# Gate and up products with the activations held in the array and their result turned by TensorE

## The chip, the cores and the metric

The kernel runs on one core of a Trainium2 chip. The metric is device time of one execution, in microseconds (us), lower is better.

## The reference, cut to what matters

One decoder layer on 256 tokens of 2048 features, all in float32: a half-weighted feed-forward block (FFN1), a mixer with a recurrent and an attention branch, a second half-weighted feed-forward block (FFN2), and a last norm.

```python
def swiglu(x, w_gate, w_up, w_down):            # 2048x5504, 2048x5504, 5504x2048
    return (jax.nn.silu(x @ w_gate) * (x @ w_up)) @ w_down

x = x + 0.5 * swiglu(rms_norm(x, ffn1_norm[l]), ffn1_w_gate[l], ffn1_w_up[l], ffn1_w_down[l])
x = x + hybrid_mixer(rms_norm(x, mix_norm[l]), w_in[l], ...)
x = x + 0.5 * swiglu(rms_norm(x, ffn2_norm[l]), ffn2_w_gate[l], ffn2_w_up[l], ffn2_w_down[l])
return rms_norm(x, final_norm)
```

## The kernel before

All sizes are in tiles of P = 128: the 2048 features are KT = 16 tiles, the 5504 hidden features NF = 43 tiles, the S = 256 tokens two halves t of 128. C = 512 is a chunk of four tiles, and NC = 4 of them make 2048.

**Two parts for each number.** Every operand of a product is split into a high part, rounded for the array's fast float32 mode, and a low part, the rest. A product is three products: high by high, high by low, low by high. `split` makes the parts with one ScalarE (ACT) and one VectorE (DVE) instruction, at L72 and L73. An activation tile with both parts beside each other is an "hl" tile, 512 columns wide for each feature tile: the high parts of 256 tokens, then the low parts. Four slots of such tiles exist (`hlp`).

**Weights.** A `Stream` loads blocks of 128x1024 floats (512 KB) from memory over SyncE's queue into one of three `raw` buffers (L88) and splits each into `whi` and `wlo`, of which there are three as well. A `raw` buffer is free for the next load once its `wlo` is made.

**Two ways to multiply.** `part` (L116, L117) holds a 128x128 weight tile in the array and moves activations through it: `whi` with 512 columns (high and low at once), then `wlo` with 256. The result stands with features on the partitions, and `total` adds its two halves. `wide` (L138 to L140) holds activations in the array, 128 tokens of one feature tile, and moves 512 columns of weights: three matmuls for each half t. The result stands with tokens on the partitions, in one PSUM bank for each t. Five banks serve such products (`mm`), three other things (`aux`).

**Where each is used.** Gate and up products of both FFNs use `part`: for each of 43 hidden tiles j, 16 pairs of matmuls for gate and 16 for up, 1,376 pairs in each FFN. Each result is then scaled by the norm (`normed`), goes through Silu, is multiplied and split, and so becomes a tile of `h`, ready for the down product, which uses `wide`. Several products of the mixer, the merge of its branches and the output projection use `wide` too. Where a result with tokens on the partitions is needed with features there, `turned` (L164) transposes it on TensorE (PE), 128x128 at a time, eight for a chunk, and the two `split` halves are made from PSUM. These transposes are put off (`later`), and `wide` runs what was put off after its feature tile k = 7 (`AFTER`). In the merge, a chunk of gates goes through a tanh on ACT (L620) while the next chunk multiplies, is combined on DVE (L720, L721) and turned in the chunk after.

**The start of FFN1.** x comes in eight transfers of two feature tiles, among them the first blocks of gate and up weights. For tile j = 0 the gate product runs as x arrives: `ready1` scales and splits one tile of x (L75, L76). The sum of squares for the norm is made from x on ACT (`add_all`, L203), added up on DVE and over partitions on PE (L222), and the factor is spread over the partitions by another PE product (`rstd`, L262). A second copy of x, with tokens on the partitions (`xt`, from `x_rows`), is loaded at j = 4 in `prepare`, into the place that x had, and is added to the result of the down product. `prepare` also holds a small PE product (L418).

**Order of work.** The program's order gives priorities; a planner orders the instructions of each engine before the run, and takes an instruction that is ready in its plan ahead of an earlier one that is not. On the chip each engine and each queue then runs in that fixed order. `held` ties an instruction to a product so that it isn't planned too early.

Of the kernel before, what the change touches and what calls it, by code (L numbers as in the profile page):

```python
# [35 lines left out]
G = 8  # L36
T1 = 8
T2 = 5
AFTER = 7
BIG = 1e30  # L40
LOWEST = -3.0e38
C = 4 * P
NC = D // C
TAKEN = -3.4e38
# [3 lines left out]
def hybrid_layer(ctx: ExitStack, tc: tile.TileContext, a, out):  # L48
# [29 lines left out]
    class Stream:  # L78


        def __init__(self, src, width=P):
            self.src, self.width, self.ahead, self.left, self.at = src, width, [], [], 0

        def load(self, parts=1):
            raw = wraw.tile([P, G * P], F32, name="raw")
            n = G * P // parts
            for i in range(parts):
                nc.sync.dma_start(raw[:, i * n:(i + 1) * n], self.src[self.at, :, i * n:(i + 1) * n])  # L88
            self.parts = parts
            self.at += 1  # L90
            self.ahead.append(raw)

        def pop(self):
            if not self.left:
                if not self.ahead:
                    self.load()
                raw = self.ahead.pop(0)
                hi = wsp.tile([P, G * P], F32R, name="whi")
                lo = wsp.tile([P, G * P], F32R, name="wlo")
                n, self.parts = G * P // self.parts, 1  # L100
                for i in range(0, G * P, n):
                    split(hi[:, i:i + n], lo[:, i:i + n], raw[:, i:i + n])
                n = self.width
                self.left = [(hi[:, i:i + n], lo[:, i:i + n]) for i in range(0, G * P, n)]
            return self.left.pop(0)
# [26 lines left out]
    def wide(ps, w, k0, k1, kts, xs, apart=0):  # L132


        def half(t, k, hi, lo):
            x = xs(k)
            xh, xl = x[:, t * P:(t + 1) * P], x[:, S + t * P:S + (t + 1) * P]
            T.matmul(ps[t], xh, hi, start=(k == 0), stop=False)  # L138
            T.matmul(ps[t], xh, lo, start=False, stop=False)  # L139
            T.matmul(ps[t], xl, hi, start=False, stop=(k == kts - 1))  # L140
# [17 lines left out]
    def turned(src, dst):  # L158

        for i in range(0, 4, 2):  # L160
            pt = aux.tile([P, 2 * S], F32, name="aux")
            for j in range(2):
                for t in range(2):
                    T.transpose(pt[:, j * S + t * P:j * S + (t + 1) * P], src(t, i + j), ident)  # L164
            dst(i, pt.rearrange("p (j s) -> p j s", j=2))
# [25 lines left out]
    class Norm:  # L191


        def __init__(self, name):
            self.name, self.acc = name, None
            self.parts = const.tile([P, NC, 2], F32, name=name)

        def add_all(self, x, after):

            sq = hl_tile("sqs", F32, (P, KT, S))  # L200
            z = held(after)
            for c in range(0, KT, 4):
                A.activation(sq[:, c:c + 4, :], x[:, c:c + 4, :], AF.Square, bias=z)  # L203
            half = KT
            while half > 2:
                half //= 2
                V.tensor_tensor(sq[:, :half, :], sq[:, :half, :], sq[:, half:2 * half, :], op=ALU.add)
            self.acc = t1("sqsum")
            V.tensor_tensor(self.acc, sq[:, 0, :], sq[:, 1, :], op=ALU.add)
# [5 lines left out]
        def sums(self):  # L215

            n = tmp.tile([P, 8], F32, name="nv")
            v, s, r = n[:, 0:2], n[:, 2:4], n[:, 4:6]
            if self.acc is not None:
                ps = aux.tile([P, 2 * S], F32, name="aux")  # L220
                for t in range(2):
                    T.matmul(ps[:, t:t + 1], self.acc[:, t * P:(t + 1) * P], mean, start=True, stop=True)  # L222
                V.tensor_scalar(v, ps[:, :2], EPS, None, op0=ALU.add)
            else:
                q = self.parts
                V.tensor_tensor(q[:, 0:2, :], q[:, 0:2, :], q[:, 2:4, :], op=ALU.add)
                V.tensor_tensor(v, q[:, 0, :], q[:, 1, :], op=ALU.add)
                V.tensor_scalar(v, v, 1.0 / D, EPS, op0=ALU.mult, op1=ALU.add)
# [47 lines left out]
    mean = const.tile([P, 1], F32, name="mean")  # L276
    GP.memset(mean, 1.0 / D)
    warm = const.tile([P, 1], F32, name="warm")
    A.activation(warm, mean, AF.Copy)
# [5 lines left out]
    def ffn(wg, wu, wd, xhl, norm, finish, ready=None, early=None):  # L285
        hs = []
        r = None

        def evacuate(j, pg, pu):
            zg = normed(pg, r)  # L290
            sg = t1("sg")
            A.activation(sg, zg, AF.Silu)
            zu = normed(pu, r)
            h = t1("h")
            V.tensor_tensor(h, zu, sg, op=ALU.mult)
            t = hs[j // KT][:, j % KT, :]
            split(t[:, :S], t[:, S:], h)

        waiting = []
        for j in range(NF):  # L300
            if j % KT == 0:
                hs.append(hl_tile("h"))
            if j == 0:
                pg, pu = psum(), psum()
                for k0 in range(0, KT, G):
                    for k in range(k0, k0 + G):
                        if ready is not None:
                            ready(k)
                        part(pg, wg, k, k + 1, KT, whole(xhl))
                    part(pu, wu, k0, k0 + G // 2, KT, whole(xhl))  # L310
                    settle()
                    part(pu, wu, k0 + G // 2, k0 + G, KT, whole(xhl))
# [5 lines left out]
            waiting.append((j, pg, pu))  # L318
            if j == 0 and ready is not None:
                norm.add_all(xr, pg)  # L320
# [4 lines left out]
            if r is not None:  # L325
                for w in waiting:
                    evacuate(*w)
                waiting = []
# [6 lines left out]
    WG1, WU1, WD1 = Stream(a["wg1"]), Stream(a["wu1"]), Stream(a["wd1"], C)  # L335
    xr = big.tile([P, KT, S], F32, name="xr", tag="f16")
# [18 lines left out]
    def ready1(c):  # L355
        spread(x1hl, c, xr[:, c, :], G1)
# [3 lines left out]
    x2hl = xt = None  # L360

    def finish1(c, ps):
# [9 lines left out]
        def gains(i, pt):  # L372
            for j in range(2):
# [8 lines left out]
    def prepare(after):  # L382
        nonlocal xt
# [39 lines left out]
    ffn(WG1, WU1, WD1, x1hl, n1, finish1, ready=ready1, early=prepare)  # L423
# [288 lines left out]
    def merge(j):  # L712
# [10 lines left out]
        def parts(i, pt):  # L723
            n = 4 * j + i
            split(mg[:, n:n + 2, :S], mg[:, n:n + 2, S:], pt)
# [11 lines left out]
    def combine(c):  # L737
# [9 lines left out]
        def gains(i, pt):  # L747
            for j in range(2):
# [34 lines left out]
    ffn(Stream(a["wg2"]), Stream(a["wu2"]), Stream(a["wd2"], C), x3hl, n3, finish2)  # L783
# [19 lines left out]
def _rows(w):  # L803

    k, n = w.shape
    t = np.asarray(w).reshape(k // P, P, n // C, C).transpose(2, 0, 1, 3).reshape(-1, G // 4, P, C)
# [56 lines left out]
```

## Time and profile before

| | |
|---|---|
| median of 3 runs | 2333.41 us (2326.3 to 2334.53) |
| profiled execution | 2324.7 us |
| its span, first to last instruction | 2322.5 us |
| TensorE busy | 2302.0 us (99%) |
| VectorE, ScalarE busy | 1438.3 us (62%), 1140.5 us (49%) |
| mean granted TensorE clock | 0.998 of full |

The profile is one execution; the rows below are from it. A matmul's printed duration reaches into the next ones, since matmuls are pipelined, so what one costs in a stream is the distance between starts. On PE in the timeline, FFN1's gate and up products run from 5.46 to 501.38 us, its down product to about 743 us, the mixer to 1599.47 us, FFN2's gate and up to 2078.17 us, and its down product to the end.

### The profile page before, as it was taken

How to read it: one execution, taken by the hardware profiler on the slowest of the kernel's cores; microseconds unless marked ns; L12 is line 12 of the kernel's file. 1: busy time of each engine (PE TensorE's matmuls, PEld its weight loads, DVE VectorE, ACT ScalarE, POOL GpSimd, SP SyncE). 2: the span in 40 equal slices, each digit the busy share in tenths (PEclk: the TensorE clock that was granted, in tenths of full speed). 3: DMA queues.
4: the chain of work that ended last, by engine and by line, in shares of the span. 5: the costliest groups of instructions: out<-in, count | busy, mean ns of one | idle time of the engine just before them, and what ended most of it. 6: DMA issues, size and time to landing. Idle time of an engine off the chain costs nothing.

```text
span 2322.5 us, 31249 instructions
## 1 busy us (share of the span) xinstructions
PE 2302.0 (99%) x11916; PEld 1956.3 (84%) x11916; DVE 1438.3 (62%) x2061; ACT 1140.5 (49%) x1603; POOL 62.3 (3%) x122
## 2 busy tenths in 40 slices
PE   8999999999999999999999999999999999999998
PEld 7888888888888888888888888888888888888886
DVE  6766666654445687766677755555666666664444
ACT  6444444444444445566655544445544444444443
POOL 0000000000000011000000000000000000000000
PEclk9999999999999999999999999999999999999999
DMA  7555555556665644456666665565555555565554
GB/s 259 187 184 189 184 188 185 189 188 199 199 200 189 213 161 149 156 184 200 206 215 208 209 208 199 200 217 186 189 190 190 189 189 189 191 208 194 194 192 162
DMA packets 130166, 448.78 MB, mean 193 GB/s; under 512 B 14896, under 2 KB 21152, under 8 KB 129632
## 3 DMA queue, kind: packets, MB, share of 16 engines
q1 hardware_dynamic: 125856, 433.89, 56.1%
q0 software_dynamic: 3984, 12.82, 1.6%
q8 instruction: 93, 1.52, 0.3%
q14 instruction: 57, 0.47, 0.1%
q10 hardware_dynamic: 176, 0.08, 0.0%
HBM read 438.25 MB, written 8.41 MB: 192 GB/s over the span
## 4 chain that ended last, share of the span: by engine, by line
PE 97%; DVE 1%; ACT 1%; issue 0%; DMA 0%; SPq 0%; DVEq 0%; ACTq 0%
PE mm L116 36%; PE mm L117 18%; PE mm L138 13%; PE mm L140 13%; PE mm L139 13%; DVE wlo L73 0%; PE aux L164 0%; PE aux L496 0%; DMA raw<-in_wu 0%; PE aux L637 0%; PE aux L638 0%; ACT whi L72 0%; PE aux L559 0%; PE aux L580 0%; PE aux L587 0%
## 5 line engine op out<-in xcount | busy, mean ns | idle before, releaser
L73 DVE TENSOR_TENSOR wlo<-raw,whi 128x1024 fp32r<-128x1024 f32 (+2 forms) x807 | 989.2, 1226 | 789.0 <-ACT whi L72 786.1
L72 ACT ACTIVATE whi<-raw 128x1024 fp32r<-128x1024 f32 (+2 forms) x807 | 854.3, 1059 | 1101.5 <-PE mm L116 423.5
L116 PE MATMUL mm<-x1hl,whi 128*128 128x512 f32 x1376 | 489.3, 400 | 7.6 <-DVE x1hl L76 7.1
L116 PE MATMUL mm<-x3hl,whi 128*128 128x512 f32 x1376 | 477.6, 391 | 0.0
L117 PE MATMUL mm<-x1hl,wlo 128*128 128x256 f32 x1376 | 387.5, 282 | 2.0 <-DVE wlo L73 2.0
L117 PE MATMUL mm<-x3hl,wlo 128*128 128x256 f32 x1376 | 385.1, 280 | 0.0
L116 PE MATMUL mm<-x2hl,whi 128*128 128x512 f32 x960 | 344.0, 401 | 0.0
L116 PEld LDWEIGHTS mm<-x1hl,whi 128*128 128x128 f32 x1376 | 259.9, 189 | 73.3 <-ACT whi L72 6.4
L116 PEld LDWEIGHTS mm<-x3hl,whi 128*128 128x128 f32 x1376 | 257.3, 187 | 56.7 <-DVE x3hl L76 0.3
L117 PE MATMUL mm<-x2hl,wlo 128*128 128x256 f32 x960 | 269.6, 281 | 0.0
L138 PE MATMUL mm<-whi,h 128*128 128x512 f32 x688 | 267.9, 389 | 0.0
L140 PE MATMUL mm<-whi,h 128*128 128x512 f32 x688 | 267.7, 389 | 0.0
L139 PE MATMUL mm<-wlo,h 128*128 128x512 f32 x688 | 267.7, 389 | 0.0
L117 PEld LDWEIGHTS mm<-x1hl,wlo 128*128 128x128 f32 x1376 | 261.2, 190 | 3.2 <-DVE wlo L73 3.0
L117 PEld LDWEIGHTS mm<-x3hl,wlo 128*128 128x128 f32 x1376 | 260.0, 189 | 0.1
L116 PEld LDWEIGHTS mm<-x2hl,whi 128*128 128x128 f32 x960 | 180.4, 188 | 44.0 <-issue 1.1
L117 PEld LDWEIGHTS mm<-x2hl,wlo 128*128 128x128 f32 x960 | 181.3, 189 | 2.3 <-issue 0.7
L140 PEld LDWEIGHTS mm<-whi,h 128*128 128x128 f32 x688 | 129.2, 188 | 26.9
L139 PEld LDWEIGHTS mm<-wlo,h 128*128 128x128 f32 x688 | 129.2, 188 | 26.8
L138 PEld LDWEIGHTS mm<-whi,h 128*128 128x128 f32 x688 | 129.2, 188 | 26.6
L138 PE MATMUL mm<-whi,x2hl 128*128 128x512 f32 x288 | 115.4, 401 | 0.0
L140 PE MATMUL mm<-whi,x2hl 128*128 128x512 f32 x288 | 112.5, 391 | 0.0
(208 smaller groups left out, 2002.3 us busy)
## 6 DMA issues: line engine op xcount, KB each, us to landing
raw<-in_wu SPq DMA_DIRECT2D x172, 512.0 KB, 4.2
raw<-in_wd SPq DMA_DIRECT2D x172, 512.0 KB, 3.4
raw<-in_wg SPq DMA_DIRECT2D x171, 512.0 KB, 4.2
raw<-in_w_q SPq DMA_DIRECT2D x32, 512.0 KB, 3.5
raw<-in_w_rx SPq DMA_DIRECT2D x32, 512.0 KB, 3.5
raw<-in_w_ga SPq DMA_DIRECT2D x32, 512.0 KB, 3.4
raw<-in_w_rg SPq DMA_DIRECT2D x32, 512.0 KB, 3.8
raw<-in_w_pa SPq DMA_DIRECT2D x32, 512.0 KB, 3.8
```

The costliest lines, as they stand in the source:

```text
L72: A.activation(hi, src, AF.Copy)
L73: V.tensor_tensor(lo, src, hi.bitcast(F32), op=ALU.subtract)
L116: T.matmul(ps, hi, x, start=(k == 0), stop=False)
L117: T.matmul(ps[:, S:], lo, x[:, :S], start=False, stop=(k == kts - 1))
L138: T.matmul(ps[t], xh, hi, start=(k == 0), stop=False)
L139: T.matmul(ps[t], xh, lo, start=False, stop=False)
L140: T.matmul(ps[t], xl, hi, start=False, stop=(k == kts - 1))
```

## The change

Gate and up products of both FFNs are made with `wide`, four hidden tiles at once (chunks at j = 0, 4, ... 36, and one of three tiles, 384 columns, at j = 40). Their weights lie in memory in the order that `wide` wants, the last three tiles in arrays of their own (`wg1b` and so on). The result has tokens on the partitions, so that the norm's factor is one number per partition: Silu takes it as its scale on ACT, and one DVE instruction scales the up product and multiplies. `turned` then transposes the result into `h`.

The first chunk's gate and up products run side by side, two feature tiles of each in turn. Of x, two tiles and the first two blocks of weights are asked for, then two more tiles and a block; the rest follows as `opening1` is called. The copy with tokens on the partitions is loaded there as well, in four pieces, and the squares for FFN1's norm are made from it. The sum over partitions and the spreading of the factor on PE are gone from both FFNs' norms. Twelve products of a tile of ones with itself stand at the head of PE's program (`IDLE`). Before, x lay in `big`, then the copy in the same place; now x lies in an `hl` slot.

```diff
@@ constants
+IDLE = 12
+WHOLE = DFF // C * C
@@ class Stream: a stream may be followed by a second, narrower one
+        def __init__(self, src, width=P, rest=None):
+            self.ahead, self.left = [], []
+            self.loads = [(src, i, width) for i in range(src.shape[0])]
+            if rest is not None:
+                self.loads += [(rest, i, rest.shape[2] // 2) for i in range(rest.shape[0])]
...
-    def turned(src, dst):
-        for i in range(0, 4, 2):
+    def turned(src, dst, tiles=4):
+        for i in range(0, tiles, 2):
+            n = min(2, tiles - i)
             pt = aux.tile([P, 2 * S], F32, name="aux")
-            for j in range(2):
+            for j in range(n):
                 for t in range(2):
                     T.transpose(pt[:, j * S + t * P:j * S + (t + 1) * P], src(t, i + j), ident)
...
@@ class Norm
-        def add_all(self, x, after):
-            sq = hl_tile("sqs", F32, (P, KT, S))
-            z = held(after)
-            for c in range(0, KT, 4):
-                A.activation(sq[:, c:c + 4, :], x[:, c:c + 4, :], AF.Square, bias=z)
...
         def sums(self):
-            if self.acc is not None:
-                ps = aux.tile([P, 2 * S], F32, name="aux")
-                for t in range(2):
-                    T.matmul(ps[:, t:t + 1], self.acc[:, t * P:(t + 1) * P], mean, start=True, stop=True)
...
+    idle = aux.tile([P, 2 * S], F32, name="aux")
+    for _ in range(IDLE):
+        T.matmul(idle[:, :P], ones, ones, start=True, stop=True)
...
@@ def ffn
-        for j in range(NF):
+        xs = whole(xhl)
+        for j in range(0, NF, 4):
             if j % KT == 0:
                 hs.append(hl_tile("h"))
             if j == 0:
...
+                pg, pu = (psum(), psum()), (psum(), psum())
+                for k in range(0, KT, 2):
+                    if opening is not None:
+                        opening(k)
+                    wide(pg, wg, k, k + 2, KT, xs)
+                    wide(pu, wu, k, k + 2, KT, xs)
+                norm.sums()
             else:
-                pg = product(wg, KT, whole(xhl))
-                if j == 1:
-                    norm.sums()
-                pu = product(wu, KT, whole(xhl))
...
-            if j == 1:
-                r = norm.rstd(pg)
+                pg = chunk(wg, KT, xs)
+            hidden(j, min(4, NF - j), pg, pu if j == 0 else None, wu, xs, norm, hs[-1])
             if j == 4 and early is not None:
-                early(pg)
...
+                early(pg[0])
...
+    def hidden(j, tiles, pg, pu, wu, xs, norm, hl):
+        n = tiles * P
+        h = [t2("h"), t2("h")]
+        for t in range(2):
+            A.activation(h[t][:, :n], pg[t][:, :n], AF.Silu, scale=norm.r[:, t:t + 1])
+        if pu is None:
+            pu = chunk(wu, KT, xs)
+        for t in range(2):
+            V.scalar_tensor_tensor(h[t][:, :n], pu[t][:, :n], norm.r[:, t:t + 1], h[t][:, :n],
+                                   op0=ALU.mult, op1=ALU.mult)
+
+        def parts(i, n, pt):
+            o = hl[:, j % KT + i:j % KT + i + n, :]
+            split(o[:, :, :S], o[:, :, S:], pt)
+
+        later.append(lambda: turned(lambda t, i: h[t][:, i * P:(i + 1) * P], parts, tiles))
...
+    WG1, WU1 = Stream(a["wg1"], C, a["wg1b"]), Stream(a["wu1"], C, a["wu1b"])
...
-    for k in range(0, KT, 2):
         nc.sync.dma_start(xr[:, k:k + 2, :], a["x"][:, k:k + 2, :])
-        if k == 0:
-            WG1.load(2)
-        if k == 6:
-            WU1.load()
+    load_x(0)
+    WG1.load(2)
+    WU1.load(2)
+    load_x(2)
+    WG1.load()
...
+    def opening1(k):
+        for c in range(k, k + 2):
+            spread(x1hl, c, xr[:, c, :], G1)
+        if k + 4 < KT:
+            load_x(k + 4)
+        i = k // 2 - 1
+        if 0 <= i < NC:
+            cs = slice(i * C, (i + 1) * C)
+            nc.sync.dma_start(xt[:, :, cs], a["x_rows"][:, :, cs])
+        i -= 1
+        if 0 <= i < NC:
+            for t in range(2):
+                n1.add(t, i, xt[:, t, i * C:(i + 1) * C])
...
     def prepare(after):
-        xt = big.tile([P, 2, D], F32, name="xt", tag="f16")
-        for t in range(2):
-            nc.sync.dma_start(xt[:, t, :], a["x_rows"][t])
...
@@ host layout
-        "wg1": _tiles(i["ffn1_w_gate"][0]),
+        "wg1": _rows(i["ffn1_w_gate"][0][:, :WHOLE]),
+        "wg1b": _rows(i["ffn1_w_gate"][0][:, WHOLE:]),
...
```

## Rows read from the trace of the kernel before

**Rows 1.** The profile's page: busy time of each engine over the span.

```profile
PE 2302.0 (99%) x11916; PEld 1956.3 (84%) x11916; DVE 1438.3 (62%) x2061; ACT 1140.5 (49%) x1603; POOL 62.3 (3%) x122
```

**Rows 2.** Timeline of PE in FFN1's gate and up products: start, duration (us), instruction.

```profile
299.63 0.40 PE L116 MATMUL mm<-x1hl,whi 128*128 128x512 f32 x1
...
303.52 0.40 PE L116 MATMUL mm<-x1hl,whi 128*128 128x512 f32 x1
...
501.38 0.40 PE L138 MATMUL mm<-whi,h 128*128 128x512 f32 x1
```

**Rows 3.** Timeline of PE where FFN2's gate and up products begin and end.

```profile
1599.47 0.39 PE L116 MATMUL mm<-x3hl,whi 128*128 128x512 f32 x1
...
2078.17 0.39 PE L138 MATMUL mm<-whi,h 128*128 128x512 f32 x1
```

**Rows 4.** Timeline of PE in FFN1's down product.

```profile
519.80 0.39 PE L138 MATMUL mm<-whi,h 128*128 128x512 f32 x1
...
522.52 0.39 PE L138 MATMUL mm<-whi,h 128*128 128x512 f32 x1
```

**Rows 5.** Chain that ended last, in order of time: start, us, what.

```profile
70.95 0.74 PE aux L418 x2
...
570.97 0.87 PE aux L164 x8
630.34 0.87 PE aux L164 x8
...
1431.03 0.87 PE aux L164 x8
1475.44 0.87 PE aux L164 x8
...
1623.05 0.45 PE aux L262 x4
```

**Rows 6.** One line's instructions (L164, transposes): duration min/median/max in ns.

```profile
L164 PE MATMUL aux<-ident,gt x32: 270/272/273, 1386.4 to 1520.5; 128*128 128x128 f32 x32
```

**Rows 7.** Groups by line in the merge, 1340 to 1520 us: busy, mean ns | idle before.

```profile
L73 DVE TENSOR_TENSOR wlo<-raw,whi 128x1024 fp32r<-128x1024 f32 x66 | 80.9, 1226 | 87.8 <-ACT whi L72 87.8
L72 ACT ACTIVATE whi<-raw 128x1024 fp32r<-128x1024 f32 x66 | 70.0, 1061 | 100.3 <-PE mm L140 98.6 <-DVE wlo L73 1.7
L138 PE MATMUL mm<-whi,yrn 128*128 128x512 f32 x128 | 49.8, 389 | 0.0
...
L620 ACT ACTIVATE gt<-mm,rh 128x512 f32<-128x512 f32 x8 | 5.5, 688 | 3.9 <-PE mm L140 3.9
...
L720 DVE SCALAR_TENSOR_TENSOR gt<-gt,mm 128x512 f32<-128x512 f32 x8 | 5.2, 681 | 0.4 <-PE mm L140 0.4
```

**Rows 8.** Timeline of PE at the start.

```profile
5.46 0.79 PE L116 MATMUL mm<-x1hl,whi 128*128 128x512 f32 x1 [5.46 <-DVE x1hl L76]
...
13.10 0.63 PE L116 MATMUL mm<-x1hl,whi 128*128 128x512 f32 x1
...
13.74 0.54 PE L116 MATMUL mm<-x1hl,whi 128*128 128x512 f32 x1
...
17.62 0.39 PE L117 MATMUL mm<-x1hl,wlo 128*128 128x256 f32 x1 [0.91 <-DVE wlo L73]
```

**Rows 9.** Timeline of ACT at the start.

```profile
4.80 0.61 ACT L72 ACTIVATE whi<-raw 128x512 fp32r<-128x512 f32 x1
6.25 0.63 ACT L72 ACTIVATE whi<-raw 128x512 fp32r<-128x512 f32 x1 [0.84 <-DMA raw<-in_wg]
8.02 2.72 ACT L75 ACTIVATE x1hl<-xr,vecs 128x256 fp32r<-128x256 f32 x6 [1.13 <-DMA xr<-in_x]
10.95 1.06 ACT L72 ACTIVATE whi<-raw 128x1024 fp32r<-128x1024 f32 x1 [0.21 <-DMA raw<-in_wu]
```

**Rows 10.** Windows at the start: the last two columns are DMA share and GB/s.

```profile
12.00:14.00 2.00, 2.00 (x8) 1.71 (x7) 1.96 (x4) 2.00 (x7) 0.00 (x0) 1.00 1.04 409
```

**Rows 11.** Groups by line, whole span: squares of 128x512.

```profile
L213 ACT ACTIVATE sq<-xn 128x512 f32<-128x512 f32 x16 | 10.0, 624 | 10.4 <-DVE xn L768 7.0 <-DVE xn L368 3.4
```

More of the change, by code (lines that the diff above doesn't have):

```diff
@@ L96, in pop @@
                     self.load()
-                raw = self.ahead.pop(0)
+                raw, n, parts, width = self.ahead.pop(0)
                 hi = wsp.tile([P, G * P], F32R, name="whi")
                 lo = wsp.tile([P, G * P], F32R, name="wlo")
-                n, self.parts = G * P // self.parts, 1
-                for i in range(0, G * P, n):
+                for i in range(0, parts * n, n):
                     split(hi[:, i:i + n], lo[:, i:i + n], raw[:, i:i + n])
-                n = self.width
-                self.left = [(hi[:, i:i + n], lo[:, i:i + n]) for i in range(0, G * P, n)]
+                self.left = [(hi[:, i:i + width], lo[:, i:i + width]) for i in range(0, parts * n, width)]
             return self.left.pop(0)
@@ L135, in half @@
         def half(t, k, hi, lo):
-            x = xs(k)
+            x, o = xs(k), ps[t][:, :hi.shape[1]]
             xh, xl = x[:, t * P:(t + 1) * P], x[:, S + t * P:S + (t + 1) * P]
-            T.matmul(ps[t], xh, hi, start=(k == 0), stop=False)
-            T.matmul(ps[t], xh, lo, start=False, stop=False)
-            T.matmul(ps[t], xl, hi, start=False, stop=(k == kts - 1))
+            T.matmul(o, xh, hi, start=(k == 0), stop=False)
+            T.matmul(o, xh, lo, start=False, stop=False)
+            T.matmul(o, xl, hi, start=False, stop=(k == kts - 1))
         for k in range(k0, k1 - apart):
@@ L282, in hybrid_layer, with ffn @@
     G1, GM, G2, CB, BA, BX, LAM = (vecs[:, i, :] for i in range(7))
-    def ffn(wg, wu, wd, xhl, norm, finish, ready=None, early=None):
+    def ffn(wg, wu, wd, xhl, norm, finish, opening=None, early=None):
         hs = []
[L287 to L299, printed above, removed]
-        for j in range(NF):
+        xs = whole(xhl)
+        for j in range(0, NF, 4):
             if j % KT == 0:
@@ L303, in ffn @@
             if j == 0:
[L304 to L312, printed above, removed]
-            else:
-                pg = product(wg, KT, whole(xhl))
-                if j == 1:
-                    norm.sums()
-                pu = product(wu, KT, whole(xhl))
@@ L370, in finish1, with gains @@
             nc.gpsimd.dma_start(x1d[c, t], xn[t])
-        def gains(i, pt):
-            for j in range(2):
+        def gains(i, n, pt):
+            for j in range(n):
                 spread(x2hl, 4 * c + i + j, pt[:, j, :], GM)
@@ L421, in prepare @@
         nc.scalar.dma_start(toep, u[:HEADS])
-    ffn(WG1, WU1, WD1, x1hl, n1, finish1, ready=ready1, early=prepare)
+    ffn(WG1, WU1, WD1, x1hl, n1, finish1, opening=opening1, early=prepare)
     xs2 = whole(x2hl)
@@ L745, in combine, with gains @@
             n3.add(t, c, new)
-        def gains(i, pt):
-            for j in range(2):
+        def gains(i, n, pt):
+            for j in range(n):
                 spread(x3hl, 4 * c + i + j, pt[:, j, :], G2)
@@ L781, in finish2 @@
             n4.most()
-    ffn(Stream(a["wg2"]), Stream(a["wu2"]), Stream(a["wd2"], C), x3hl, n3, finish2)
+    ffn(Stream(a["wg2"], C, a["wg2b"]), Stream(a["wu2"], C, a["wu2b"]), Stream(a["wd2"], C), x3hl, n3, finish2)
 def _buckets():
@@ L824 @@
                                    "rg_b_a", "rg_b_x", "rg_lambda")], axis=1)),
-        "x_rows": np.ascontiguousarray(i["x"][0].reshape(2, P, D)),
+        "x_rows": np.ascontiguousarray(i["x"][0].reshape(2, P, D).transpose(1, 0, 2)),
         "gains": np.ascontiguousarray(i["final_norm"]).reshape(1, D),
```

75 lines of the change are left out of this document (29 added, 46 removed).

## Prediction

> **What bounds the kernel now.** I read the page first: PE is busy for 2302 of 2322.5 us [rows 1]. The reader should see that nothing but PE's stream of matmuls, and the few places where it stands still, can move the time. A busy PE says nothing of its pace, so I then read the timeline for the distance between starts. In FFN1's gate and up products eleven pairs take 303.52 - 299.63 = 3.89 us, 353.6 ns a pair of 512 + 256 columns [rows 2]. In FFN2 the whole stage takes 478.70 us [rows 3]; without the 0.87 us of transposes and 0.45 us of L262 that lie in it [rows 5], 477.38 / 1376 = 346.9 ns a pair. In the down product twelve matmuls of 512 columns take 2.72 us, 226.7 ns each [rows 4]. So 768 columns cost 353.6 or 346.9 ns by `part` and 1.5 x 226.7 = 340.1 ns by `wide`: the columns are the same, the pace is not. Last I read the start, where PE waits and runs slowly.
>
> **The steady part.** The change moves as many columns as before. For 1,376 pairs the other form saves 1376 x 13.5 ns = 18.6 us in FFN1 and 1376 x 6.8 = 9.4 us in FFN2, if gate and up run at the pace of the down product. I take that pace because two other stages show it: the distance of two groups of transposes is 59.37 us for 258 matmuls in the down product and 44.41 us for 192 in the merge [rows 5]; less 0.87 both give 226.7 ns, with other operands held and moved. It is bounded above by FFN2's present pace per column, 231.3 ns, and below by nothing faster than 226.7. The 384-column matmuls of the last chunk don't occur before; I take 0.75 x 226.7 = 170 ns, and at FFN2's rate they would be 173 (0.7 us for 192 of them).
>
> **What is added on PE.** Ten chunks are turned with eight transposes each and the last with six: 86 in each FFN. Eight cost 0.87 us in the chain [rows 5], so 10 x 0.87 + 0.65 = 9.35 us for each FFN, 18.7 us in all. This takes back two thirds of the gain. One transpose's row lasts 272 ns [rows 6], but the next starts before it ends, so I take the chain's 109 ns and keep 272 for a rival. The Trainium skill ("TensorE: Matmul & The Clock Gate", "Part 4: PE-mode transpose") gives about 275 ns for a transpose among other work; the trace agrees as to the duration and not as to what eight of them take. By that figure the transposes would cost 47.3 us and the change would lose some 16 us.
>
> **The stages summed.** FFN1: the first chunk has 192 matmuls, 43.53 us. Nine chunks follow, each like one round of the merge (96 + 96 matmuls, eight transposes), 44.41 us: 399.7. The last has 192 matmuls of 384 columns and the eight transposes of the chunk before, 33.5. L418 stays, 0.74 [rows 5]. The last six transposes fall into the down product, 0.65. Sum 478.1 us, against 501.38 - 5.46 = 495.92 now [rows 2, 8]; the products L222 and L262 are gone from the new sum. What of these 17.8 us remains depends on the start. FFN2: 43.53 + 399.7 + 33.5 + 0.65 + 0.87 (transposes of the stage before, as now) = 478.25 against 478.70: 0.45 us gained.
>
> **Evacuation.** Before, 43 tiles went through `total`, scaling, Silu, product and split; now Silu is two ACT instructions of 128x512 on PSUM for a chunk (0.69 us each, as L620), the product two of DVE (0.68, as L720), and the split as in the merge [rows 7]. Both engines do less than before. I cost this at nothing, covered by 21.8 us of matmuls for each 96. If the cover failed, the price is that of the rival on ACT's queue below. PE needs two of five banks for each product; the banks of the gate product come free after Silu, a product's time before they are wanted.
>
> **The start.** Now 16 pairs of the gate product want all of x early. PE starts at 5.46; until 13.74 its pairs start 0.64 us apart (13.10 to 13.74), which for 768 columns is the lower clock of 1.2 GHz, though the clock's record in these windows reads 1.00 [rows 8, 10]; it waits again before 17.62 for a `wlo`. The Trainium skill ("TensorE: Matmul & The Clock Gate", "Part 1: The HAM clock gate") has the clock start low and rise with sustained work, which these rows fit. The twelve products at the head are there in that stretch. Two plain float32 products take 0.45 us at the higher clock [rows 5], so twelve take 2.7 us, or 5.4 at the lower one. Begun at the head of the program, within the first microsecond, they may hold the first matmul up by 0.9 us; I cost that at nothing, since PE waits for data anyway, as follows.
>
> In the new order the first seven transfers of SP's queue have the sizes of the first seven now: six of 256 KB and one of 512. Now the second is split at 4.80, the third at 6.25, the fourth used at 8.02 and the seventh at 10.95 [rows 9]. So gate's two half blocks come at 4.8 and 6.2, up's at 8.0 and some 9, x's second pair at 9.7, and the next gate block at 10.9 (the fifth and sixth are estimates between the fourth and the seventh). PE's first 24 matmuls, 5.44 us, then end at about 11.9 instead of 10.9. The block of 10.9 is split by 12.0 (1.06 us) and its low part by 13.3 (1.23) [rows 7]; one matmul runs between, eleven after: 15.8. The up block behind it waits for its buffer and, in the program's order, behind two more pairs of x and 512 KB of `x_rows`: 1 MB at 409 GB/s [rows 10] is 2.6 us, so it lands at 10.9 + 2.6 + 1.3 = 14.8, is split by 17.1, and PE is done with 48 matmuls at 19.7. Without waits that were 5.46 + 10.88 = 16.3. So the start loses 3.4 us at least, and 5.4 if the planner takes another pair of x and piece of `x_rows` (0.77 MB, 1.9 us) first. After that blocks come in time: 1 MB of weights, 0.25 of x and 0.5 of `x_rows` for each 5.44 us are 337 GB/s against 409. The squares are eight of 0.62 us [rows 11]; what they add up to is wanted only at the chunk's end. One that waits for its piece of `x_rows` holds up the splits behind it on ACT, but the first piece is due at 13.5 and squared two pairs of tiles later. Streams, the host's layout and the norm's own tile cost nothing on the chip. I add 1 us for waits that I can't place and take 5.4 us. Upper bound: the planner, which fills SP's time with whatever is ready, puts all the rest of x and `x_rows` (2.6 MB, 6.4 us) ahead of that block, and the clock stays low until then (a matmul then takes two thirds of 0.64 us, and 48 end 2.1 us later): 3.4 + 6.4 + 2.1 = 12 us.
>
> **The sum.** FFN1: 495.92 - 478.1 - 5.4 = 12.4 us gained; FFN2: 0.45. Together 12.9 us: span 2309.6 instead of 2322.5, and 2311.8 instead of 2324.7 for the execution. The profiled execution lies 8.7 us under the median of the runs shown, 2333.41; from that median the forecast is 2320.5 us. That is 0.55% faster, and a measurement of this kernel can tell about 0.5% (11.7 us) from no change.
>
> **Rivals.**
> A start that loses more: 8 to 12 us as in the upper bound, so that 6 to 10 remain: 2323 to 2327 us. For it: all these transfers are ready from the first moment, and the weights' buffers aren't; against it: x and its copy stand behind blocks of weights in the program's order.
> The start loses less, or stages in the mixer that are planned anew run closer: 15 to 18 us gained, 2315 to 2318.
> The form brings no better pace (slower): if gate and up kept their own time per column, the 28.0 us fall away, and the transposes stay: 12.9 - 28.0 = -15.1, 2348.5 us. It eats the gain once the 4,128 matmuls take 3.1 ns more each, 229.8 on the mean. Against it stand the two stages of [rows 4, 5]. The Trainium skill ("TensorE: Matmul & The Clock Gate", "Back-to-back issue gap") would have it nearly so: columns at 2.4 GHz and 2.5 ns for a matmul make 325.0 ns for a pair and 323.7 for 1.5 matmuls of 512, and the change would lose 11.5 us. No row here shows those times.
> Transposes at their full duration: 172 x (272 - 109) ns = 28 us more, 2348.6 us. Against it: two rounds of eight, 0.87 us each, in the chain.
> ACT's queue (slower): at each of 22 handovers from gate to up, Silu waits for the product's last matmul; if the plan puts it before the next block's split, PE waits up to 0.69 + 1.06 = 1.75 us, 38 us in all, 2359 us. It eats the gain from 0.59 us a handover. Against it: the merge has the same shape with L620, and PE's groups there show no idle time [rows 7].
>
> **Chances and range.** The forecast, with a start that loses 3.4 to 8 us: 0.50. The longer start 0.25, the larger gain 0.10, the pace 0.05, the transposes 0.03, ACT's queue 0.07. A gain over 11.7 us needs a start that loses under 6.6: 0.38 of the first, with the larger gain 0.48. Slower by over 0.5%: 0.05 + 0.03 + 0.04 of the last = 0.12. The rest, 0.40, is within 0.5%. The range: below, 15 us under the profiled execution, 2309, as the runs of one kernel lie from there to 2334.5; above, FFN2's pace per column in both (4.6 ns x 4128 = 19 us lost, 2339.5), cut to what leaves out 1 in 10, 2336.
>
> **What would show it.** In the new trace: 226.7 ns between starts of 512-column matmuls with `x1hl` and `x3hl`, and 44.4 us from one group of transposes to the next through both FFNs; 0.87 us for eight. The 48th matmul of the start near 19.7 us, and the down product of FFN1 begun near 488.4. No idle time of PE at the handovers. FFN2's stage unchanged within 1 us. The prediction is wrong if PE waits later than about 25 us into the span, if any of these paces is off by 1%, or if the mixer's 856 us, which the change doesn't touch, move by some microseconds with the new plan.

## The result, and the profile after

The changed kernel takes 2313.28 us (median of 6 runs, 2312.14 to 2314.44); the kernel before, run beside it, 2333.61 us (median of 6, 2326.3 to 2334.96). The ratio is 0.9916, with an interval of 0.9903 to 0.9929; by the medians it is 20.3 us or 0.87% faster. The forecast was 2320.5 us, within its range, and 7.2 us too high.

The profiled execution took 2312.14 us with a span of 2310.0 us; the forecast for its span was 2309.6. So the profile gained 12.5 us, as forecast, and the median 20.3. Where the other 8 us come from is the question of this study.

The page of the changed kernel, busy time of each engine, beside [rows 1]:

```profile
PE 2295.2 (99%) x10820; PEld 1920.1 (83%) x10820; DVE 1293.7 (56%) x1633; ACT 1091.4 (47%) x1366; POOL 62.1 (3%) x121
```

PE runs 1,096 instructions fewer (640 matmuls fewer in each FFN, 172 transposes and the products at the head more) and is still the bound. The timeline of PE where the two stages end or begin (start, duration in us, instruction), beside [rows 2, 3]:

```profile
488.54 0.39 PE L141 MATMUL mm<-whi,h 128*128 128x512 f32 x1
...
1586.22 0.39 PE L141 MATMUL mm<-whi,x3hl 128*128 128x512 f32 x1
...
2064.54 0.39 PE L141 MATMUL mm<-whi,h 128*128 128x512 f32 x1
```

FFN1's down product begins at 488.54 us (501.38 before), what lies between takes 1097.68 us (1098.09), and FFN2's gate and up 478.32 us (478.70). What follows from there to the end takes 1.1 us more than before, 0.66 of it the last six transposes. By this profile nearly all was gained in FFN1.

The chain that ended last, in order of time (start, us, what), beside [rows 5]:

```profile
110.10 0.87 PE aux L168 x8
154.51 0.87 PE aux L168 x8
198.93 0.87 PE aux L168 x8
...
499.63 0.66 PE aux L168 x6
```

L168 is the transpose in `turned`. The rounds lie 44.41 us apart, which less 0.87 is 226.8 ns for each of 192 matmuls.

The start, in PE's timeline of the changed kernel (in brackets the idle time before an instruction and what ended it), beside [rows 8]; L141 to L143 are the three matmuls of `wide`:

```profile
11.79 0.62 PE L141 MATMUL mm<-whi,x1hl 128*128 128x512 f32 x2
12.89 0.50 PE L142 MATMUL mm<-wlo,x1hl 128*128 128x512 f32 x1 [0.47 <-DVE wlo L75]
...
16.24 0.73 PE L141 MATMUL mm<-whi,x1hl 128*128 128x512 f32 x2 [0.79 <-ACT whi L74]
17.50 0.50 PE L142 MATMUL mm<-wlo,x1hl 128*128 128x512 f32 x1 [0.53 <-DVE wlo L75]
...
19.89 0.61 PE L141 MATMUL mm<-whi,x1hl 128*128 128x512 f32 x2
20.83 0.50 PE L142 MATMUL mm<-wlo,x1hl 128*128 128x512 f32 x1 [0.32 <-DVE wlo L75]
...
32.23 0.50 PE L142 MATMUL mm<-wlo,x1hl 128*128 128x512 f32 x1 [0.23 <-DVE wlo L75]
```

The 49th matmul starts at 19.89 us, where the forecast had it (19.7). After it come two waits more, at 20.83 and 32.23. The second has its cause on ACT, whose timeline is:

```profile
28.46 0.63 ACT L204 ACTIVATE sq<-xt 128x512 f32<-128x512 f32 x1 [1.79 <-DMA xt<-in_x_rows]
...
29.86 1.06 ACT L74 ACTIVATE whi<-raw 128x1024 fp32r<-128x1024 f32 x1
```

A square waited 1.79 us for the fourth piece of `x_rows`; the split of a weight block came behind it on ACT at 29.86, and PE wanted that block's low part at 32.23. The square did not hold the split up. SyncE asked for the block at 22.30, behind that piece, and it landed 7.5 us later, at 29.8 (its issue on SyncE's queue, then the view of DMA issues: KB, us to landing):

```profile
22.30 0.54 SPq L95 DMA_DIRECT2D raw<-in_wg  x1
...
raw<-in_wg SPq DMA_DIRECT2D x1, 512.0 KB, 7.5
```

The longer waits before 16.24 and 17.50 have the same cause: the up block asked for at 6.96, behind the first piece of `x_rows`, landed 8.1 us later, and its split begins at 15.13.

### The profile page after: what moved, and what is told of

Same layout as the page of the kernel before. It is cut to its first block, busy times and chain, and to the rows that moved or that the text cites. A ratio compares the mean times of both kernels' runs of the same rounds, so it can differ in the third digit from the quotient of the medians.

```text
span 2310.0 us, 28338 instructions
## 1 busy us (share of the span) xinstructions
PE 2295.2 (99%) x10820; PEld 1920.1 (83%) x10820; DVE 1293.7 (56%) x1633; ACT 1091.4 (47%) x1366; POOL 62.1 (3%) x121
## 4 chain that ended last, share of the span: by engine, by line
PE 97%; DVE 1%; DMA 1%; ACT 1%; issue 0%; SPq 0%; DVEq 0%; ACTq 0%
PE mm L142 27%; PE mm L143 27%; PE mm L141 27%; PE mm L119 9%; PE mm L120 5%; PE aux L168 1%; DMA xt<-in_x_rows 1%; DVE wlo L75 0%; PE aux L487 0%; PE aux L628 0%; PE aux L629 0%; DMA raw<-in_wu 0%; ACT whi L74 0%; PE aux L550 0%; PE aux L571 0%
## 5 line engine op out<-in xcount | busy, mean ns | idle before, releaser
L142 PE MATMUL mm<-wlo,x1hl 128*128 128x512 f32 (+1 forms) x704 | 271.0, 385 | 1.7 <-DVE wlo L75 1.5
L141 PE MATMUL mm<-whi,x1hl 128*128 128x512 f32 (+1 forms) x704 | 270.8, 386 | 0.8 <-ACT whi L74 0.8
L141 PE MATMUL mm<-whi,x3hl 128*128 128x512 f32 (+1 forms) x704 | 271.3, 385 | 0.0
L143 PE MATMUL mm<-whi,x1hl 128*128 128x512 f32 (+1 forms) x704 | 270.5, 384 | 0.0
L143 PE MATMUL mm<-whi,x3hl 128*128 128x512 f32 (+1 forms) x704 | 270.4, 384 | 0.0
L142 PE MATMUL mm<-wlo,x3hl 128*128 128x512 f32 (+1 forms) x704 | 270.4, 384 | 0.0
L141 PE MATMUL mm<-whi,h 128*128 128x512 f32 x688 | 268.1, 390 | 0.0
L143 PE MATMUL mm<-whi,h 128*128 128x512 f32 x688 | 267.7, 389 | 0.0
L142 PEld LDWEIGHTS mm<-wlo,x1hl 128*128 128x128 f32 x704 | 132.2, 188 | 28.4 <-DVE wlo L75 3.9
L141 PEld LDWEIGHTS mm<-whi,x1hl 128*128 128x128 f32 x704 | 132.1, 188 | 26.5 <-ACT whi L74 1.2
L143 PEld LDWEIGHTS mm<-whi,x3hl 128*128 128x128 f32 x704 | 132.2, 188 | 24.9
L143 PEld LDWEIGHTS mm<-whi,x1hl 128*128 128x128 f32 x704 | 132.2, 188 | 24.7
L141 PEld LDWEIGHTS mm<-whi,x3hl 128*128 128x128 f32 x704 | 132.2, 188 | 24.6
L142 PEld LDWEIGHTS mm<-wlo,x3hl 128*128 128x128 f32 x704 | 132.2, 188 | 24.6
```

What stands on the lines that cost most here:

```text
L141: T.matmul(o, xh, hi, start=(k == 0), stop=False)
L142: T.matmul(o, xh, lo, start=False, stop=False)
L143: T.matmul(o, xl, hi, start=False, stop=(k == kts - 1))
```

## The experiments

Each kernel was run beside the kernel before on the same chip; ratios are to that.

### The kernel before, profiled once more

Nothing is edited. [Rows 2, 3] show one code at two paces in one execution, 353.6 ns a pair in FFN1 and 346.9 in FFN2. The question is whether FFN2 always has the shorter one.

> The kernel before, unchanged, profiled once more. Theory A: its 512 + 256 pairs run at one of two paces, 346.7 or 353.4 ns, and in most executions FFN2's gate and up products run at the slower one, in the profiled execution at the faster: 1376 x 6.5 ns = 9 us, the distance of that execution (2324.7 us) to the median (2333.6). Then times near 2333.5 us with some near 2325, and a profile whose time is near 2333 has FFN2's stage at 487 to 488 us in place of 478.7 and all other stages as before. Theory B: the profiled execution was quicker for another reason, in the start, in the mixer or outside the span: FFN2's stage stays at 478.7 us, and 8 us are found elsewhere.

Measured: median 2333.47 us of 12 runs (2325.71 to 2334.77): one at 2325.7, the others at 2333.2 to 2334.8. The profiled execution took 2333.2 us, 8.5 us more than the one profiled before. PE's timeline of it:

```profile
1599.02 0.39 PE L116 MATMUL mm<-x3hl,whi 128*128 128x512 f32 x1
...
1799.79 0.40 PE L116 MATMUL mm<-x3hl,whi 128*128 128x512 f32 x1
...
1803.33 0.40 PE L116 MATMUL mm<-x3hl,whi 128*128 128x512 f32 x1
...
2086.70 0.40 PE L138 MATMUL mm<-whi,h 128*128 128x512 f32 x1
```

Ten pairs of FFN2 take 3.54 us, 354 ns each, and the stage takes 2086.70 - 1599.02 = 487.68 us instead of 478.70. FFN1's down product begins at 500.88 us, as in [rows 2]. The 9.0 us of this one stage account for the difference of the two executions. The two groups of times in the runs of the kernel before, about 2325 and 2334 us, fit this, with one execution of each group profiled: 6 of the 30 runs beside the first four experiments lay below 2327, 7 of 15 beside the next four, and none of 7 beside the last two. The profile that the prediction was made from was one of the shorter ones.

### FFN1 alone in the new form, and FFN2 alone

```diff
@@ the changed kernel, FFN2 in the form of before
-    ffn(Stream(a["wg2"], C, a["wg2b"]), Stream(a["wu2"], C, a["wu2b"]), ..., x3hl, n3, finish2)
+    ffn_old(Stream(a["wg2"]), Stream(a["wu2"]), ..., x3hl, n3, finish2)
@@ the kernel before, FFN2 in the new form
-    ffn(Stream(a["wg2"]), Stream(a["wu2"]), ..., x3hl, n3, finish2)
+    ffn_new(Stream(a["wg2"], C, a["wg2b"]), Stream(a["wu2"], C, a["wu2b"]), ..., x3hl, n3, finish2)
```

> FFN1 as changed, FFN2 as before. Both theories: FFN1's stage ends near 488.5 us, 12.4 us sooner than in the first profile. Theory A: 2321 us (FFN2 still at the slower pace in most executions, stage 487 us in a profile of such a time), ratio 0.9947. Theory B: the whole 20 us came with FFN1 (a gain that the profiled execution of the kernel before hides), 2313.5 us, ratio 0.9915.

Measured with FFN1 alone: 2322.08 us (2320.95 to 2322.97, 7 runs), ratio 0.9958 (0.9944 to 0.9973), 11.4 us gained against 2333.43, the median of the 30 runs beside it. In its profile FFN2's pairs ran at the longer pace and the stage took 487.7 us. FFN1's down product begins at 490.0 us, 1.5 later than in the changed kernel: the start is the same code there, and its 193rd matmul starts at 55.13 us for 53.67. So much the start differs from one execution to the next.

> FFN2 as changed, FFN1 as before. Theory A: 0.45 us by the first profile and 9 us more since the pace of FFN2's stage is 226.7 ns a matmul in every execution: 2324 us, ratio 0.996, and little spread among its runs. Theory B: 2333 us, ratio 1.000 (FFN2's stage 478.3 for 478.7).

Measured with FFN2 alone: 2325.94 us (2318.21 to 2329.17, 12 runs), ratio 0.9969 (0.9954 to 0.9985), 7.5 us gained on the median. In its profile FFN2's stage took 478.6 us and FFN1's pairs ran at 353.3 ns. The level is as expected. That the runs would lie close together was wrong: four took 2318.2 to 2319.6 us and eight 2325.6 to 2329.2. With FFN2 out of the question, pairs are left in FFN1 (1,376) and in the mixer (960). The groups' medians lie some 9 us apart, and 960 x 6.7 ns are only 6.4, so FFN1 is the likelier place; no execution of the shorter group was profiled, so that is argued, not shown.

The two halves, 11.35 + 7.49 = 18.8 us, make up most of the 20.3 us of the whole. So FFN2, from which the forecast expected 0.45 us, gave 7.5.

### A plain product behind L418

In the profile of before, FFN2's pairs run at the shorter pace and FFN1's at the longer. The pair stream is broken in few places, by plain float32 products such as L418 and L262. This kernel adds one more (of zeros, used nowhere) behind L418.

```diff
@@ the kernel before, in prepare, after L418
+        d = t1("nudge")
+        V.tensor_scalar(d[:, :P], ident, z, None, op0=ALU.mult)
+        pn = aux.tile([P, 2 * S], F32, name="aux")
+        T.matmul(pn[:, :P], ones, d[:, :P], start=True, stop=True)
```

> The kernel before, with one plain float32 product of full size (128x128, a tile of zeros) right behind L418 in FFN1. In the first profile FFN1's pairs went from 346.6 to 353.4 ns behind L418, a product with 32 rows, and FFN2's ran at 346.9 behind the full-size L164 and L262. Theory A1: a full-size plain product brings the faster pace back: FFN1's stage ends 1218 x 6.6 ns = 8.0 us sooner, less 0.2 for the product, near 493.6 us, and the kernel runs 7.8 us faster, ratio 0.9967. Theory A2: the pace falls out by chance at any interruption of the stream and such a product has no say: FFN1's pairs stay at 353.4 ns, or change without regard to it; ratio 1.000 on the mean.

Measured: 2325.2 us (2324.04 to 2332.17, 12 runs, 11 of them at 2324.0 to 2326.5), ratio 0.9971 (0.996 to 0.9982). PE's timeline of it in FFN2:

```profile
1612.71 0.40 PE L116 MATMUL mm<-x3hl,whi 128*128 128x512 f32 x1
...
1623.31 0.40 PE L116 MATMUL mm<-x3hl,whi 128*128 128x512 f32 x1
...
1623.67 0.60 PE L262 MATMUL aux<-diag,ones 128*128 128x128 f32 x4
...
1624.47 0.39 PE L116 MATMUL mm<-x3hl,whi 128*128 128x512 f32 x1
...
1628.28 0.39 PE L116 MATMUL mm<-x3hl,whi 128*128 128x512 f32 x1
```

FFN1 behind the added product stayed at 353.3 ns, so the theory by which a full-sized plain product there brings FFN1 the shorter pace falls. In FFN2 thirty pairs take 10.60 us ahead of L262, 353.3 ns each, and eleven take 3.81 us behind it, 346.4 each: the pace changed there. That the pace can change at a break stands. Why this kernel draws the shorter pace in FFN2 in 11 of 12 runs stays open.

### A break after each of FFN2's hidden tiles

```diff
@@ the kernel before, in hidden tile j, after its split
+            if ready is None:
+                pn = aux.tile([P, 2 * S], F32, name="aux")
+                T.matmul(pn[:, :P], ones, h[:, :P], start=True, stop=True)
```

The added product's result is used nowhere.

> The kernel before with a plain float32 product of full size (128x128, result unused) after each of FFN2's 43 hidden tiles: 10 to 20 us slower for these products alone. Theory A2: every such interruption of the stream of pairs draws the pace anew: FFN2's stretches between two of them show 346.7 ns in some and 353.3 in others. Rival: the pace belongs to the execution or the stage and no interruption within it changes it: all stretches of FFN2 alike.

Measured: one execution of 2342.39 us, span 2340.1. PE's timeline at one place of the first stretch and around two of the breaks:

```profile
1607.92 0.90 PE L116 MATMUL mm<-x3hl,whi 128*128 128x512 f32 x2
1608.65 0.40 PE L117 MATMUL mm<-x3hl,wlo 128*128 128x256 f32 x2
...
1684.62 0.49 PE L300 MATMUL aux<-h,ones 128*128 128x128 f32 x2
...
1687.85 0.39 PE L116 MATMUL mm<-x3hl,whi 128*128 128x512 f32 x1
...
1695.82 0.39 PE L116 MATMUL mm<-x3hl,whi 128*128 128x512 f32 x1
1696.11 0.49 PE L300 MATMUL aux<-h,ones 128*128 128x128 f32 x2
...
1696.91 0.40 PE L116 MATMUL mm<-x3hl,whi 128*128 128x512 f32 x1
...
1706.81 0.40 PE L116 MATMUL mm<-x3hl,whi 128*128 128x512 f32 x1
```

Behind the first break 23 pairs take 7.97 us, 346.5 ns each; behind the second 28 take 9.90 us, 353.6. Of 41 stretches between breaks that are long enough to tell (19 pairs or more), 31 ran at the shorter pace, 9 at the longer, and one, the first of the stage, was mixed. Within the other 40 the pace did not change. The mixed one changes at 1607.92, where no product breaks it: there the planner's order has two matmuls of 512 columns and then two of 256 (the first two lines). Its pairs start 346.6 ns apart before that and 353.4 after. The same place changed the pace in the second profile of the kernel before and in that of the kernel with a product behind L418, and did not in the first profile of the kernel before. So a break, or a change in the order of lengths, can draw the pace anew, and in these stretches the stream kept it until the next one. What decides the draw is open.

### Pairs made even: three matmuls of 256 columns

The pair's 512 columns are cut in two, so that all matmuls have one length and no alternation is left; the columns and the sums are the same.

```diff
@@ the kernel before, part()
-            T.matmul(ps, hi, x, start=(k == 0), stop=False)
+            if k == 0:
+                T.matmul(ps, hi, x, start=True, stop=False)
+            else:
+                T.matmul(ps[:, :S], hi, x[:, :S], start=False, stop=False)
+                T.matmul(ps[:, S:], hi, x[:, S:], start=False, stop=False)
             T.matmul(ps[:, S:], lo, x[:, :S], start=False, stop=(k == kts - 1))
```

> The kernel before, where every pair of 512 + 256 columns (but the first of each product) is made three matmuls of 256: the same columns and the same layout, no transposes, weights still held in the array, one more weight load for each pair. Theory A: the two paces come from the lengths that alternate, and the change's gain is even lengths, not what is held: 3 x 113.4 = 340 ns for 768 columns, about 13 ns less for some 3,500 pairs: 45 us faster, 2288 us, and little spread. Theory B: each matmul has a price of some 3.4 ns: 3 x 116.7 = 350 ns, 10 us faster. Theory C: matmuls of 256 can't hide a weight load each (its rows last 188 ns): 128 ns or more a matmul, 384 for the three, 110 us slower.

Measured: 2358.58 us (2357.47 to 2358.98, 5 runs), ratio 1.0123 (1.0102 to 1.0145), 25.6 us slower by the medians. No theory had the size, and only the one that expected 110 us more had the sign. PE's timeline of it in FFN1:

```profile
299.72 0.28 PE L119 MATMUL mm<-x1hl,whi 128*128 128x256 f32 x1
299.84 0.28 PE L120 MATMUL mm<-x1hl,whi 128*128 128x256 f32 x1
299.96 0.29 PE L121 MATMUL mm<-x1hl,wlo 128*128 128x256 f32 x1
...
303.20 0.28 PE L121 MATMUL mm<-x1hl,wlo 128*128 128x256 f32 x1
```

29 matmuls take 3.48 us, 120.0 ns each and 360 ns for 768 columns. Beside it stand 512 columns at 226.7 ns [rows 4], and the changed kernel's last chunk of 384 columns:

```profile
469.82 0.33 PE L141 MATMUL mm<-whi,x1hl 128*128 128x384 f32 x1
...
472.08 0.33 PE L142 MATMUL mm<-wlo,x1hl 128*128 128x384 f32 x1
```

These 13 take 2.254 us in the trace's nanoseconds, 173.4 ns each. From 256 to 512 columns 106.7 ns are added, 2.4 columns a ns, and what is left is nearly the same at all three lengths: 120.0 - 106.7 = 13.3, 173.4 - 160.0 = 13.4 and 226.7 - 213.3 = 13.4 ns. A matmul here costs its columns at 2.4 GHz and about 13.3 ns. Then 768 columns cost 320 + 2 x 13.3 = 346.6 ns as a pair, 320 + 3 x 13.3 = 360 in three, and 320 + 1.5 x 13.3 = 340.0 in the form of the change. The pair's shorter pace is what this sum gives; the longer one has 6.7 ns on top, for which no run shows a cause.

### Every transpose of gate and up made twice

```diff
@@ the changed kernel, turned(), called with times=2 by hidden()
-                for t in range(2):
+                for t in [0, 1] * times:
                     T.transpose(...)
```

> The changed kernel with every transpose of a hidden tile made twice into the same place: 172 more. Theory A: a transpose holds PE for 109 ns, 0.87 us for eight: 18.7 us more, 2332 us. Rival: its whole row of 272 ns once it stands among others: 46.8 us more, 2360 us.

Measured: 2332.75 us (2331.43 to 2333.23, 10 runs), 19.5 us above the changed kernel, 113 ns for each of 172 more transposes. The chain of this kernel:

```profile
112.23 1.75 PE aux L168 x16
157.52 1.75 PE aux L168 x16
```

Sixteen take 1.75 us, 109 ns each; the rest of the 19.5 us is no more than the start differs (the 193rd matmul starts at 54.90 here). The rival that each costs its printed 272 ns falls.

### The head of the program: no products of ones

```diff
@@ the changed kernel
-    for _ in range(IDLE):
-        T.matmul(idle[:, :P], ones, ones, start=True, stop=True)
```

> The changed kernel without the twelve products at the head. Theory A: PE runs at the lower clock (0.43 us between 512-column matmuls) until about 13.7 us, as in the kernel before, but mostly in time that it would wait for the second up block anyway: 19 matmuls done by 13.7, the 24th at 14.9 for 11.8, the 48th near 20.3 for 19.9, and 0.4 us lost in all, at most 1: 2313.7 us. Rival: the waits of the start keep the clock low for longer, to 20 us or more, and the 48th matmul ends 3 to 5 us later: 2317 us.

Measured: 2313.66 us (2312.25 to 2313.74, 4 runs), span 2311.4. The 49th matmul starts at 20.32 us, as expected (19.89 in the changed kernel), and the 193rd at 54.80. That the lower clock would last until about 13.7 us was wrong. PE's timeline of this kernel:

```profile
9.59 0.63 PE L142 MATMUL mm<-whi,x1hl 128*128 128x512 f32 x1
10.02 0.57 PE L140 MATMUL mm<-whi,x1hl 128*128 128x512 f32 x1
10.42 0.39 PE L141 MATMUL mm<-wlo,x1hl 128*128 128x512 f32 x1
10.65 0.39 PE L142 MATMUL mm<-whi,x1hl 128*128 128x512 f32 x1
```

Until about 10.4 us starts of 512 columns lie 0.43 us apart, 1.2 columns a ns, the lower level of 1.2 GHz; then 0.23. In the changed kernel they are 0.23 apart from the third matmul on, save where PE waits. The products cover 4.7 us of slow clock here, but the loads set the pace of the start anyway. The medians differ by 0.4 us, the runs of the two kernels overlap (2312.14 to 2314.44 with the products), and the 193rd matmul lies between 53.67 and 55.13 in the three profiles whose start has them (the changed kernel, FFN1 alone, every transpose twice). So no worth of the products is shown.

### The pieces of `x_rows` two pairs of tiles later

```diff
@@ the changed kernel, opening1()
-        i = k // 2 - 1
+        i = k // 2 - 3
         if 0 <= i < NC:
             cs = slice(i * C, (i + 1) * C)
             nc.sync.dma_start(xt[:, :, cs], a["x_rows"][:, :, cs])
```

> The changed kernel with each piece of the second copy of x asked for, and squared, two pairs of feature tiles later. Theory A: the start's loss of 4.7 us is the second up block standing behind 512 KB of the copy on the queue, and squares on ACT waiting for their piece (1.79 us before the one at 28.46) with a split behind them; with both out of the way PE's 48th matmul ends near 18.6 for 19.9 and the later wait at 32.2 goes: 1.5 to 2 us faster, 2311.5 us. Rival: the block waits for its buffer and PE for the split in any order: 2313.3 us, no change.

Measured: 2310.93 us (2310.76 to 2311.99, 4 runs), ratio 0.9921 (0.9897 to 0.9945); its slowest run is faster than the fastest of the changed kernel (2312.14). The 49th matmul starts at 18.22 us, the 193rd at 51.61 (53.67 to 55.13 in the three profiles of the other order), and the down product at 486.49. PE's waits in this kernel and before it in the changed one (us in total, times, longest):

```profile
PE aux L266 <- POOL ones L260: 1.0, 1, 1.0
PE mm L142 <- DVE wlo L75: 0.8, 2, 0.4
```

```profile
PE mm L142 <- DVE wlo L75: 1.5, 4, 0.5
PE aux L266 <- POOL ones L260: 1.0, 1, 1.0
PE mm L141 <- ACT whi L74: 0.8, 1, 0.8
```

The waits before 16.24 and 17.50 are gone. The up block behind them is asked for at 7.41 and lands 5.9 us later, at 13.3 for 15.1. The expectation had a second cause, a split held up on ACT by a waiting square; the landing times of the changed kernel show none. The copy of x is wanted only at the end of the first chunk, so it is cheap to let weights pass. This version is faster than both kernels.

### The first chunk's gate ahead of its up

```diff
@@ the changed kernel, ffn()
                     wide(pg, wg, k, k + 2, KT, xs)
-                    wide(pu, wu, k, k + 2, KT, xs)
```

The up product follows the whole gate product, as in the other chunks.

> The changed kernel with the first chunk's gate product made alone, its up product after it, the loads of the start as they are. Theory A: side by side is worth what x's supply is worth: the gate product alone wants 0.5 MB of weights, 0.25 MB of x and 0.5 MB of the second copy for each 2.72 us, 470 GB/s, more than the 409 that the queue gave; its 8.4 MB then end near 26 us for 21.8 us of matmuls, and the start loses 2 to 4 us more: 2315.3 to 2317.3 us. Rival: PE waits for x's own pieces and their splits one by one, as in the kernel before: 6 us more or above. Other rival: no loss, 2313.3 us, as the up blocks that are loaded first only stood in the way.

Measured: 2319.32 us (2319.16 to 2319.83, 4 runs), 6.0 us above the changed kernel; the 193rd matmul starts at 60.74 us, 7.1 us later. The larger price was nearer, though not by its cause: it named x's pieces, and PE's waits are for splits of weights. PE's timeline of it:

```profile
11.99 0.73 PE L141 MATMUL mm<-whi,x1hl 128*128 128x512 f32 x2 [2.38 <-ACT whi L74]
13.25 0.63 PE L142 MATMUL mm<-wlo,x1hl 128*128 128x512 f32 x1 [0.53 <-DVE wlo L75]
13.68 0.63 PE L143 MATMUL mm<-whi,x1hl 128*128 128x512 f32 x1
...
16.67 0.50 PE L142 MATMUL mm<-wlo,x1hl 128*128 128x512 f32 x1
17.01 0.39 PE L143 MATMUL mm<-whi,x1hl 128*128 128x512 f32 x1
```

PE waits 6.3 us for splits of weights in all (2.3 in the changed kernel), and behind the first long wait the starts lie 0.43 us apart until 16.67: the clock had fallen to its lower level.

## Why the prediction was right or wrong

**The steady part: right in pace, for this form.** 226.7 ns for 512 columns was taken from the down product and the merge, and both FFNs run at it: 44.41 us from round to round. The rival that the form brings no better pace falls, and the forecast that was worked out from the Trainium skill's 2.5 ns for a matmul ("TensorE: Matmul & The Clock Gate", "Back-to-back issue gap", where it is the gap of a lone matmul) falls with it: the runs show 13.3 ns at 256, 384 and 512 columns. That price, paid 1.5 times for 768 columns instead of twice, is 6.7 ns of gain a pair, all of it where the pairs ran at 346.7. Where they ran at 353.3 another 6.7 ns come from leaving the longer pace, and that half of the gain has a size but no known cause. The 384-column matmuls were taken at three quarters of 226.7, 170 ns, and take 173.4: 0.65 us in each FFN, since the 13.3 ns do not shrink with the columns. Beside the first profile of before, FFN2 therefore gained nothing: 478.32 us and 0.66 for its last six transposes are 0.28 more than 478.70, where 0.45 less was forecast.

**The term that was mis-sized: FFN2's gain of 1376 x 6.8 = 9.4 us.** It came from FFN2's 346.9 ns a pair, read from one execution. In most executions FFN2 runs at the same longer pace as FFN1: (487.68 - 1.32) / 1376 = 353.5 ns, 13.4 over the new form's 340.1, and the term is 18.4 us. The prediction had the hint in its first paragraph, 353.6 and 346.9 ns for the same code, and the spread of the three runs (2326.3 to 2334.53) beside a profiled execution of 2324.7; it took the pace for a property of the stage and carried the profile's gain over to the median. With 9.0 us more (487.68 - 478.70) the gain from the median is 12.9 + 9.0 = 21.9, which gives 2311.5 us; measured were 2313.28, and the profiled execution of the changed kernel lies 1.1 us under its median. The agreement of the profile's 12.5 us with the forecast's 12.9 is in part luck: it rests on one execution of the kernel before that happened to be of the shorter group.

**The transposes: right.** 0.87 us for eight and 0.66 for six; 172 more of them cost 19.5 us where the prediction's sum gives 18.7 and the full duration 46.8. The Trainium skill's 275 ns ("TensorE: Matmul & The Clock Gate", "Part 4: PE-mode transpose") is the duration that the rows show too, 272, but not what one adds to a stream, 109.

**Evacuation: right.** PE's list of waits has none at a handover from gate to up; the rival of ACT's queue falls. Silu takes 690 ns, as the tanh of [rows 7].

**The start: right within 1 us, one step wrong.** The first 24 matmuls end near 11.8 us (forecast 11.9) and the 49th starts at 19.89 (19.7). The 193rd starts at 53.67; begun at 5.46 without waits it would be 48.99, so the start loses 4.7 us (5.4 taken). The 5.4 is not the sum of its terms: 3.4 and 1 for waits without a place are 4.4, and with the other pair of x and piece of `x_rows` first they are 6.4. That loss is of one profile; in two others with the same start it is 5.9 and 6.1. The mechanism was as forecast up to the second up block, which was forecast to land at 14.8 behind x and `x_rows` and landed at 15.1. The step that failed is "After that blocks come in time": two waits came later, at 20.83 and at 32.23, the second past the 25 us that the prediction gave as a sign of being wrong. Its mean of 337 GB/s against 409 did not say when a single block lands, and the block behind the fourth piece of `x_rows` took 7.5 us. That squares waiting for `x_rows` cost next to nothing was right. Moving the loads gives back 2.1 us at the 193rd matmul. The order of loads was worth looking at, and the warm-up products hardly.

**The mixer.** From FFN1's down product to FFN2 0.4 us were gained, although six transposes (0.66 us) were added there, so the rest gained 1.1. Of that 0.7 us are one stretch of 104 pairs, which ran at 346.7 ns in the profile of the changed kernel and at 353.3 in that of the kernel before: a drawn pace, and no effect of the change that a run shows.

## What to carry to other kernels

When one trace shows the same code at two paces, or the profiled execution lies at the edge of the runs' times, ask which executions the profile speaks for, and profile another before a gain is worked out from it: here a stage differed by 9.0 us from one execution to the next. Count the matmuls a column needs, not only the columns: the same 768 columns cost 340, 347 (or 353) or 360 ns in 1.5, 2 or 3 matmuls. At the start, a load that is wanted late is issued late: moving four pieces of the second input behind weights gave 2.35 us.

## What the runs showed of the hardware

A matmul of these operands costs its columns at 2.4 GHz and about 13.3 ns, at 256, 384 and 512 columns. A stream of alternating 512 and 256 columns runs at 346.7 or 353.3 ns a pair; plain float32 products between them break it, behind each break it runs at either (31 and 9 of 40 stretches) and holds that. In three profiles the pace changed without such a product as well, where two matmuls of 512 columns and two of 256 follow each other. `wide`, all of one length, had 226.7 ns in both FFNs of every profile that uses it there. What decides between the two paces is not known from these runs.

The clock's level after a wait: behind a wait of 2.38 us it was at 1.2 GHz until 16.67 us (above), and behind the changed kernel's wait of 0.79 us before 16.24 it was not: from 18.07 to 19.21 us six starts there lie 0.23 us apart on the mean.
